# Moving a store ahead of y in one in-order queue of transfers

One core of a Trainium2 chip runs the kernel. The metric is the device time of that core in microseconds (us); lower is better.

## The reference

```python
def setup_inputs():
    batch, m, k, n = 16, 512, 768, 1024
    return {"x": randn(batch, k, m), "y": randn(batch, k, n)}   # float32

def reference(x, y):
    return np.einsum('bkm,bkn->bmn', x, y).astype(np.float32)
```

Sixteen products of a 512 x 768 by a 768 x 1024 matrix: 75.5 MB are read and 33.55 MB written.

## The kernel before

One batch entry is a round. The sync engine issues all transfers; VectorE casts x and y to bf16; PE multiplies (48 matmuls in two groups); ScalarE copies each group out of PSUM.

```python
LAG = 4          # the store of round b - 4 is issued in round b
NO = 5           # output buffers; xs, ys, xb, yb and the PSUM groups have two each
...
def store(b):
    if b < B - 2:
        nc.sync.wait_ge(groups, 2 * (b + 2))      # matmuls of round b + 1 done
    else:
        nc.sync.wait_ge(outs, b - (B - 3))        # copies of round b done
    nc.sync.dma_start(o_v[b], ob[b % NO][:]).then_inc(so[b % NO], 16)

for b in range(B):
    i = b % 2
    if b >= 2:
        nc.sync.wait_ge(cast, nx[b - 2])          # x of round b - 2 cast: its buffer is free
    wide_dma("x", xs[i][:], x_v[b], 4, True).then_inc(sx[i], 16)
    if b >= 2:
        nc.sync.wait_ge(cast, nx[b - 2] + parts(b - 2))
    wide_dma("y", ys[i][:], y_v[b], 2, True).then_inc(sy[i], 16)
    if b >= LAG:
        store(b - LAG)
for b in range(B - LAG, B):
    store(b)
...
# VectorE, round b
    if b >= 2:
        nc.vector.wait_ge(groups, 2 * (b - 1))    # xb and yb of round b - 2 read
    nc.vector.wait_ge(sx[i], n)
    nc.vector.tensor_copy(xb[:, i], xs[i][:]).then_inc(cast, 1)
    nc.vector.wait_ge(sy[i], n)
    nc.vector.tensor_copy(yb[:, i], ys[i][:]).then_inc(cast, 1)   # the last y in two halves
...
# ScalarE, round b, group g (cut here: from b = 5 on it first waits until the store of round b - 5 has landed)
    nc.scalar.wait_ge(groups, 2 * b + g + 1)
    cp = nc.scalar.copy(ob[b % NO][:, ...], ps[g][:])             # the last one releases the last store
```

Of the kernel before, what the change touches and what calls it, by code (L numbers as in the profile page):

```python
# [1 line left out]

_os.environ.setdefault("NEURON_RT_ULTRASERVER_MODE", "4")

# [2 lines left out]

# [5 lines left out]


@with_exitstack
def kernel(
    ctx: ExitStack,
    tc: tile.TileContext,
    x: bass.AP,
    y: bass.AP,  # L20
    out: bass.AP,
):
    nc = tc.nc
    P = 128
    FP32 = mybir.dt.float32
    BF16 = mybir.dt.bfloat16

    B, K, M = x.shape
    _, _, N = y.shape
    KT = K // P  # L30
    MT = M // P
    NF = 512
    NT = N // NF



    x_v = x.rearrange("b (p ko) m -> b p ko m", ko=KT)
    y_v = y.rearrange("b (p ko) n -> b p ko n", ko=KT)
    o_v = out.rearrange("b (p mo) n -> b p mo n", mo=MT)

    LAG = 4
    NO = 5
    KH = KT // 2

    ctx.enter_context(tc.tile_critical())
    ec = ctx.enter_context
    xs = [ec(nc.sbuf_tensor(f"xs{i}", [P, KT, M], FP32)) for i in range(2)]
    ys = [ec(nc.sbuf_tensor(f"ys{i}", [P, KT, N], FP32)) for i in range(2)]
    xb = ec(nc.sbuf_tensor("xb", [P, 2, KT, M], BF16))
    yb = ec(nc.sbuf_tensor("yb", [P, 2, KT, N], BF16))  # L50
    ob = [ec(nc.sbuf_tensor(f"ob{i}", [P, MT, N], FP32)) for i in range(NO)]

    HB = MT // 2
    ps = [ec(nc.psum_tensor(f"ps{i}", [P, HB, NT, NF], FP32)) for i in range(2)]
    sx = [ec(nc.semaphore(f"sx{i}")) for i in range(2)]
    sy = [ec(nc.semaphore(f"sy{i}")) for i in range(2)]
    so = [ec(nc.semaphore(f"so{i}")) for i in range(NO)]
    cast = ec(nc.semaphore("cast"))
    ready = ec(nc.semaphore("ready"))
    room = ec(nc.semaphore("room"))  # L60
    groups = ec(nc.semaphore("groups"))
    idle = ec(nc.semaphore("idle"))
    outs = ec(nc.semaphore("outs"))


    made = {}

    def wide_dma(key, dst, src, dram_rows, load):


        if key not in made:
            made[key] = nc.sync.dma_start(dst, src)
            return made[key]
        pat = mybir.BassSymbolicTensorAccessPattern
        widen = lambda a: a.rearrange("(q r) k m -> q (r k m)", r=dram_rows)
        plain = lambda a: a.rearrange("p k m -> p (k m)")
        s, d = (widen(src), plain(dst)) if load else (plain(src), widen(dst))
        return nc.sync.add_instruction(_copy.replace(
            made[key].ins, name=nc.get_next_instruction_name(),
            ins=(pat(ap=s.ap, dtype=s.dtype, bass_ap=s, is_dma=False),),  # L80
            outs=(pat(ap=d.ap, dtype=d.dtype, bass_ap=d, is_dma=False),),
            sync_info=None, ant_dge_precooked=False))


    def parts(b):
        return 2 if b in (15,) else 1


    nx = [sum(1 + parts(a) for a in range(b)) + 1 for b in range(B)]


    def store(b):


        if b < B - 2:
            nc.sync.wait_ge(groups, 2 * (b + 2))
        else:
            nc.sync.wait_ge(outs, b - (B - 3))
# [4 lines that stand above are left out]
        if b >= 2:  # L103
            nc.sync.wait_ge(cast, nx[b - 2])
        wide_dma("x", xs[i][:], x_v[b], 4, True).then_inc(sx[i], 16)
        if b >= 2:
            nc.sync.wait_ge(cast, nx[b - 2] + parts(b - 2))
        wide_dma("y", ys[i][:], y_v[b], 2, True).then_inc(sy[i], 16)
        if b >= LAG:
            store(b - LAG)  # L110
    for b in range(B - LAG, B):
        store(b)


    for _ in range(60):
        nc.vector.sem_inc(idle, 1)
    for b in range(B):
        i = b % 2
        n = 16 * (b // 2 + 1)
        if b >= 2:  # L120
            nc.vector.wait_ge(groups, 2 * (b - 1))
# [3 lines that stand above are left out]
        for h in range(parts(b)):  # L125
            ks = slice(h * KT // parts(b), (h + 1) * KT // parts(b))
            nc.vector.tensor_copy(yb[:, i, ks], ys[i][:, ks]).then_inc(cast, 1)  # L127


    for b in range(B):  # L130
        nc.gpsimd.wait_ge(cast, nx[b]).then_inc(ready, 1)
        for h in range(parts(b)):
            nc.gpsimd.wait_ge(cast, nx[b] + h + 1).then_inc(ready, 2 // parts(b))


    x_w = xb[:].rearrange("p s k (j mo) -> p s k mo j", mo=MT)
    pe = OrderedEngineSet([nc.tensor.engine])
    with nc.Fori(0, B // 2, engines=pe):
        with nc.Fori(0, 2, engines=pe) as s:
            nc.tensor.wait_ge(ready, 2).then_inc(ready, -2)  # L140
            for mo in range(MT):
                g, m = divmod(mo, HB)
                if m == 0:
                    nc.tensor.wait_ge(room, 1).then_inc(room, -1)  # L144
                for kt in range(KT):
                    if mo == 0 and kt == KH:
                        nc.tensor.wait_ge(ready, 1).then_inc(ready, -1)
                    for nt in range(NT):
                        mm = nc.tensor.matmul(  # L149
                            ps[g][:, m, nt], x_w[:, bass.ds(s, 1), kt, mo],  # L150
                            yb[:, bass.ds(s, 1), kt, nt * NF:(nt + 1) * NF],
                            start=(kt == 0), stop=(kt == KT - 1))
                if m == HB - 1:
                    mm.then_inc(groups, 1)


    nc.scalar.nop().then_inc(room, 2)
    for _ in range(60):
        nc.scalar.sem_inc(idle, 1)
    for b in range(B):  # L160
        if b >= NO:
            nc.scalar.wait_ge(so[b % NO], 16 * (b // NO))
        for g in range(2):
            nc.scalar.wait_ge(groups, 2 * b + g + 1)
            cp = nc.scalar.copy(ob[b % NO][:, g * HB:(g + 1) * HB].rearrange("p m (t f) -> p m t f", f=NF),  # L165
                                ps[g][:])
            if b < B - 1:
                cp.then_inc(room, 1)
        if b == B - 2:
            nc.scalar.drain().then_inc(outs, 1)  # L170
    cp.then_inc(outs, 1)

    for i in range(NO):
        nc.sync.wait_ge(so[i], 16 * len(range(i, B, NO)))


# [1 line left out]
_INS = ['x', 'y']  # L178
_OUTS = [((16, 512, 1024), 'float32')]


# [23 lines left out]
```

## Time and profile before

| | before |
|---|---|
| median time, first comparison | 262.54 us (262.36 to 262.94, 4 runs) |
| span of the profiled run | 260.2 us |
| share of the 16 DMA engines' span | 98.3% |
| busy PE / VectorE / ScalarE | 72% / 32% / 23% |
| last y lands / last copy ends / end | 234.7 / 251.2 / 260.2 us |

The order of issue of one middle round, from the timeline of the sync engine in the kernel before (start us, us, engine, line, operation):

```profile
181.84 0.47 SPq L72 DMA_DIRECT2D xs<-in_x_dram  x1
190.66 0.47 SPq L72 DMA_DIRECT2D ys<-in_y_dram  x1
191.18 0.59 SPq L99 DMA_DIRECT2D out_dram<-ob  x1
```

The store follows y at once: its own wait was over when the matmuls of round 11 ended, at 187.58 us.

### The profile page before, as it was taken

What the parts mean: (1) busy time and instruction counts of PE and PEld (TensorE: products, weight loads), DVE (VectorE), ACT (ScalarE), POOL (GpSimd) and SP (SyncE); (2) the same over time, 40 slices, a digit from 0 to 9 for tenths busy, and PEclk for the clock granted to TensorE, in tenths of its full rate; (3) what the DMA queues carried; (4) which work ended last, traced back from release to release, by engine and by line L of the source; (5) the groups of instructions that cost most, each with busy time, mean ns of one, the idle gap of its engine ahead of it and who ended that gap; (6) DMA issues with size and microseconds to landing.
All of it is one profiled execution on the core that took longest, in us unless ns stands there. A gap on an engine that the chain in (4) does not pass through costs nothing. (4 is left out here: it accounts for less than half of the span.)

```text
span 260.2 us, 2506 instructions
## 1 busy us (share of the span) xinstructions
PE 188.3 (72%) x768; PEld 90.3 (35%) x768; DVE 82.0 (32%) x33; ACT 61.1 (23%) x33; POOL 0.2 (0%) x4
## 2 busy tenths in 40 slices
PE   0019999998938959499491995949869697785930
PEld 0004555554513525244250352514424243442410
DVE  0261644525241152511425214252232523125000
ACT  1000442243220222203222022220412204031220
POOL 0000000000000000000000000000000000000000
PEclk9999999999995979979999597997968989997985
DMA  7999989999999999999999999999999999999995
GB/s 272 418 476 408 476 378 469 393 368 461 438 398 469 388 479 423 411 441 393 458 431 441 433 388 464 408 436 446 396 456 418 464 416 423 451 385 431 438 403 227
DMA packets 4514, 109.07 MB, mean 419 GB/s; under 512 B 768, under 2 KB 768, under 8 KB 768
## 3 DMA queue, kind: packets, MB, share of 16 engines
q1 hardware_dynamic: 4512, 109.05, 98.3%
q14 instruction: 2, 0.02, 0.0%
HBM read 75.50 MB, written 33.55 MB: 419 GB/s over the span
## 5 line engine op out<-in xcount | busy, mean ns | idle before, releaser
L149 PE MATMUL ps<-yb,xb 128*128 x768 | 188.3, 411 | 61.0 <-PEq L144 61.0
L149 PEld LDWEIGHTS ps<-yb,xb 128*128 x768 | 90.3, 118 | 158.5 <-issue 92.6
L165 ACT COPY ob<-ps 128x2048 f32<-128x2048 f32 x32 | 59.8, 1869 | 184.8 <-PE ps L149 184.8
L127 DVE CAST yb<-ys 128x6144 bf16<-128x6144 f32 (+1 forms) x17 | 53.8, 3171 | 86.5 <-DMA ys<-in_y_dram 86.5
L123 DVE CAST xb<-xs 128x3072 bf16<-128x3072 f32 x16 | 28.2, 1760 | 69.7 <-DMA xs<-in_x_dram 65.2
L165 ACT ACT_TABLE_LOAD x1 | 1.3, 1283 | 5.3 <-issue 5.3
L189 POOL MEMSET const-bfloat16-1.0<- 128x1 bf16 x1 | 0.1, 102 | 0.0
L189 POOL MEMSET const-uint8-127<- 128x1 uint8 x1 | 0.1, 102 | 0.0
L189 POOL MEMSET const-float32-1.0<- 128x1 f32 x1 | 0.1, 99 | 0.0
L189 POOL MEMSET const-float32-0.0<- 128x1 f32 x1 | 0.1, 98 | 0.2 <-issue 0.2
## 6 DMA issues: line engine op xcount, KB each, us to landing
ys<-in_y_dram SPq DMA_DIRECT2D x16, 3072.0 KB, 28.2
out_dram<-ob SPq DMA_DIRECT2D x16, 2048.0 KB, 32.6
xs<-in_x_dram SPq DMA_DIRECT2D x16, 1536.0 KB, 29.8
```

The costliest lines, as they stand in the source:

```text
L123: nc.vector.tensor_copy(xb[:, i], xs[i][:]).then_inc(cast, 1)
L127: nc.vector.tensor_copy(yb[:, i, ks], ys[i][:, ks]).then_inc(cast, 1)
L149: mm = nc.tensor.matmul(ps[g][:, m, nt], x_w[:, bass.ds(s, 1), kt, mo], yb[:, bass.ds(s, 1), kt, nt * NF:(nt + 1) * NF], start=(kt == 0), ...
L165: cp = nc.scalar.copy(ob[b % NO][:, g * HB:(g + 1) * HB].rearrange("p m (t f) -> p m t f", f=NF), ps[g][:])
L189: nc = _bacc.Bacc("TRN2", target_bir_lowering=False, num_devices=1)
```

## The change

The intent is to let the store go as soon as its data is there, between x and y, rather than behind y's wait for a free buffer.

```diff
         wide_dma("x", xs[i][:], x_v[b], 4, True).then_inc(sx[i], 16)
+        if LAG <= b < B - 1:
+            store(b - LAG)
         if b >= 2:
             nc.sync.wait_ge(cast, nx[b - 2] + parts(b - 2))
         wide_dma("y", ys[i][:], y_v[b], 2, True).then_inc(sy[i], 16)
-        if b >= LAG:
+        if b == B - 1:
             store(b - LAG)
```

## The prediction

> **What bounds the kernel now.** I read the page's DMA rows first, because a core that moves 109 MB in 260 us is suspected of being bound by transfers.
>
> ```profile
> DMA  7999989999999999999999999999999999999995
> q1 hardware_dynamic: 4512, 109.05, 98.3%
> HBM read 75.50 MB, written 33.55 MB: 419 GB/s over the span
> ```
>
> All 48 transfers go through one queue, and their packets occupy the 16 DMA engines for 98.3% of the span. Only the first and the last slice are visibly lower. PE is busy 72%, DVE 32%, ACT 23%: none is close. The chain that ended last holds only the last 48 matmuls (12.25 us) and one copy (1.87 us), because it doesn't follow queued transfers; I don't take it for the bound.
>
> Next, whether the queue ever runs dry. The issue table has the time from issue to landing:
>
> ```profile
> ys<-in_y_dram SPq DMA_DIRECT2D x16, 3072.0 KB, 28.2
> out_dram<-ob SPq DMA_DIRECT2D x16, 2048.0 KB, 32.6
> xs<-in_x_dram SPq DMA_DIRECT2D x16, 1536.0 KB, 29.8
> ```
>
> A transfer is issued about 30 us before it lands. A round (one x, one y, one store: 1.573 + 3.146 + 2.097 = 6.816 MB) takes 15.8 us, so nearly two rounds wait in the queue. The sync engine's waits for casts (115.8 us for y, 66.7 us for x) are therefore harmless: they hold up issues, not data. Stretches that begin where y landed, and three at the end, confirm it (columns: length, busy time of the five engines, granted clock, DMA share, GB/s):
>
> ```profile
> core 0: us, PE busy (x) PEld busy (x) DVE busy (x) ACT busy (x) POOL busy (x), PEclk, DMA share, GB/s
> 171.46:187.27 15.81, 12.02 (x49) 5.73 (x48) 5.12 (x2) 3.74 (x2) 0.00 (x0) 0.89 1.00 432
> 187.27:203.08 15.81, 12.23 (x45) 5.32 (x44) 5.12 (x3) 3.73 (x2) 0.00 (x0) 0.78 1.01 432
> ...
> 250.00:251.00 1.00, 0.00 (x0) 0.00 (x0) 0.00 (x0) 1.00 (x1) 0.00 (x0) 1.00 0.99 426
> 251.00:252.00 1.00, 0.00 (x0) 0.00 (x0) 0.00 (x0) 0.19 (x1) 0.00 (x0) 0.78 0.65 279
> 252.00:257.00 5.00, 0.00 (x0) 0.00 (x0) 0.00 (x0) 0.00 (x0) 0.00 (x0) 0.50 0.99 419
> ```
>
> The steady rounds run at share 1.00 and 432 GB/s. The one hole after the start-up is at 251 us: share 0.65, some 0.35 us lost. That is where the last store is issued. The timeline of the last two rounds:
>
> ```profile
> 211.68 1.76 DVE L123 CAST xb<-xs 128x3072 bf16<-128x3072 f32 x1 [5.24 <-DMA xs<-in_x_dram]
> ...
> 218.90 3.36 DVE L127 CAST yb<-ys 128x6144 bf16<-128x6144 f32 x1 [5.46 <-DMA ys<-in_y_dram]
> ...
> 222.83 10.55 PE L149 MATMUL ps<-yb,xb 128*128 x48 [3.63 <-PEq L144]
> 227.50 1.76 DVE L123 CAST xb<-xs 128x3072 bf16<-128x3072 f32 x1 [5.24 <-DMA xs<-in_x_dram]
> ...
> 237.05 12.23 PE L149 MATMUL ps<-yb,xb 128*128 x48 [3.67 <-PEq L144]
> ...
> 249.33 1.87 ACT L165 COPY ob<-ps 128x2048 f32<-128x2048 f32 x1 [3.25 <-PE ps L149]
> ```
>
> The start of a cast is here the landing of its input. The last y lands at 234.7; five stores of 4.99 us remain, ready in time except the last, issued at 251.2 when the last copy ends, just about when the queue runs out. So the kernel is bound by bytes throughout, and the last matmuls and copy are all but co-critical.
>
> [...] 432 in a steady round, and y alone at 3.146 MB / 7.22 us = 436. [...] x, y, store land in the order of issue. [...] in the trace 48 matmuls after a gap take 10.55 us in 2 rounds of 11, about 12.2 in 6, and 13.1 to 13.5 in 3, the granted clock falling to 0.50 for some microseconds.
>
> **The change part by part.** It adds and removes no instruction: 16 x, 16 y and 16 stores remain, each of the same shape. For rounds 4 to 14 it moves 11 stores from behind y to ahead of y. Round 15 and the last four stores keep their order.
>
> 1. Bytes and switches. Still 109.05 MB. The queue went x y s x y s; it becomes x s y x s y, still one group of loads and one store in turn, the same number of changes of direction. Gain: 0.
>
> 2. Issue waits. The store of round b-4 waits for the matmuls of round b-3. Now y of round b stands behind that wait. Take times relative to the landing of x of round b-2. From x to y are 7.22 us, from y to the next x 8.60; the x part of that is 3.61 at y's rate, so a store takes 4.99. In the new order y lands at 4.99 + 7.22 = 12.21, its cast ends at 15.57, and the next y may be issued. Matmuls of a round start some 0.5 us after y's cast (222.26 to 222.83) and take at most 13.5, so those of round b-3 end by 15.57 + 0.5 + 13.5 - 15.82 = 13.8. The store goes at 11 to 13.8, ahead of 15.57: it costs y no issue time. Issue to landing of y remains about 28 us, so even a missed microsecond would be hidden. Cost: 0.
>
> 3. Buffers. y and hence the matmuls come 5 us later in each middle round. The x cast of round b needs the matmuls of round b-2 finished: by 29.6 against a landing at 31.64 (two rounds). At worst 2.0 us are left. The output buffers are freed no later than before. Cost: 0.
>
> 4. First store. It waits until 41.74 in the trace; y4 was issued at 40.29 and is now issued behind it, at about 42.2. y3 landed at 47.89 and x4 after it, so y4 has more than 5 us in hand. Cost: 0.
>
> 5. The end. Up to y of round 15 the same bytes are ahead of it, so it again lands at 234.7. But y14 lands at 218.90 + 4.99 = 223.89, its cast ends at 227.25 (just before x15 lands at 227.50), and round 14's matmuls start at about 227.8 instead of 222.83. They end at 238.4, 240.0 or 241.2 with 10.55, 12.2 or 13.4 us. Round 15 was ready at 237.05; now it waits for PE, starts without a gap and at full clock (two copies lie 5.18 us apart in the early, uninterrupted rounds: 10.37 us for 48). It ends at 248.8, 250.4 or 251.6, and with 1.87 us of copy the last store is issued at 250.7, 252.3 or 253.5, against 251.2.
>
> Its landing takes 7.7 us in the trace, some of it behind the store before it. With an empty queue I estimate [...] 1.6 from the last byte (about 257.3) to landing (258.9): 7.0 us. So the end moves by -0.35 at best (the hole, which is all that can be filled), by +0.4 to +1.1 in the middle case, by +1.6 to +2.3 in the worst. Weighted 2:6:3 with centres -0.3, +0.75 and +1.95: about +0.9 us.
>
> Sum: 0 + 0 + 0 + 0 + 0.9 on 262.55 gives 263.4. [...] y periods now vary from 15.81 to 16.17 us between 75 and 171 us (about 1.4 us in all) for a reason I don't see; that could come out either way. I say 263.2.
>
> **Rivals.** (a) The store, now earlier, evens out the traffic and removes those 1.4 us and the hole: 260.8. For it: the rounds at 15.81 show the rate that is possible. Against: the share stays 1.00 in the slow rounds too, and reads and writes alternate as before. [...]
> (b) The store's wait for PE blocks the queue: each round PE's end, y's issue and the next matmuls would form a loop, and a round would lose microseconds, 11 rounds of 1 us making 273. For it: the chain y, matmuls, store, y is now in one queue. Against: step 2, with nearly 30 us between issue and landing; the loop spans two rounds and has slack.
> (c) PE slips past its slack [...] and the end is as in the worst case of step 5: 264.7.
>
> **Range and chances.** The middle is fixed by bytes, the tail may give -0.35 to +2.3, and the unexplained variation is worth about 1.4 either way: 261.6 to 265.0. A change of 2% is 5.25 us; [...] slower needs (b). 0.02, 0.94, 0.04.
>
> **What would show it.** Right: queue share near 98%, period of x landings 15.8 to 16.0, x to y about 12.2 and y to x about 3.6 us, y15 landing near 234.7, rounds 14 and 15 back to back on PE, the last store issued at 250.7 to 253.5 and a deeper hole before it if late. Wrong: DMA share below 0.95 in a middle round, issue to landing of y well under 20 us, or steady rounds whose rate differs from 432 GB/s though the queue is full.

What no trace of this case showed is cut above, where it is marked. In step 5 two terms of the last store's landing on an empty queue, with the 1.6 us, came to 7.0 us, and the +0.9 us of step 5, the sum of 263.4 and the point of 263.2 us were reckoned with the two; these were the author's assumption. The trace of before has 0.64 us from the end of the first issue (1.34 us) to the first packet (1.98 us), and at the 436 GB/s of y alone 2.097 MB take 4.81 us. What sets the granted clock of a round is not shown (after a gap of 3.63 us 48 matmuls took 10.55 us at a clock of 1.00, after one of 3.58 us 13.38 us at 0.78).

Two readings of the trace of before that the prediction uses, with their figures: all 48 transfers land in the order of issue (the last part of each; the first of them at 7.20 us, the last at 258.93 us), and "full clock" in step 5 is the granted clock of 1.00 from 26.22 to 62.43 us, where PE has no gap.

## The result and the profile after

| first comparison | before | after |
|---|---|---|
| median of 4 runs, us | 262.54 | 263.20 (263.03 to 263.59) |
| ratio (95% interval) | | 1.0025 (1.0008 to 1.0042) |
| last y's cast starts | 234.72 | 236.15 |
| last copy ends | 251.20 | 251.93 |
| span | 260.2 | 261.6 |

A ratio is the mean time of one kernel's fast runs over that of the other's of the same rounds, so it is not quite the ratio of the medians quoted.

The page of the kernel after: its span, the DMA rows, and the issue table with the time from issue to landing.

```profile
span 261.6 us, 2506 instructions
...
DMA  6998999999999999989999998999999999999994
...
q1 hardware_dynamic: 4512, 109.05, 97.9%
...
ys<-in_y_dram SPq DMA_DIRECT2D x16, 3072.0 KB, 28.2
out_dram<-ob SPq DMA_DIRECT2D x16, 2048.0 KB, 24.1
xs<-in_x_dram SPq DMA_DIRECT2D x16, 1536.0 KB, 29.8
```

By these times the queue is as full as before: y and x wait in it as long as before (28.2 and 29.8 us). The store waits 8.5 us less (32.6 to 24.1), as it now waits for PE on the issuing engine instead of in the queue: the sync engine's waits for PE ahead of stores add up to 130.2 us, against 26.8 before. A middle round on the sync engine, kernel after:

```profile
183.09 0.47 SPq L72 DMA_DIRECT2D xs<-in_x_dram  x1
193.73 0.34 SPq L99 DMA_DIRECT2D out_dram<-ob  x1
196.77 0.47 SPq L72 DMA_DIRECT2D ys<-in_y_dram  x1
```

The last rounds, from the timeline of the kernel after. The start of a cast is the landing of its input (the last y lands at 236.13 us, its cast starts at 236.15), except where VectorE was still busy.

```profile
213.07 1.76 DVE L125 CAST xb<-xs 128x3072 bf16<-128x3072 f32 x1 [0.46 <-DMA xs<-in_x_dram]
...
225.18 3.36 DVE L129 CAST yb<-ys 128x6144 bf16<-128x6144 f32 x1 [10.35 <-DMA ys<-in_y_dram]
...
228.94 1.76 DVE L125 CAST xb<-xs 128x3072 bf16<-128x3072 f32 x1 [0.40 <-DMA xs<-in_x_dram]
229.11 20.91 PE L151 MATMUL ps<-yb,xb 128*128 x96 [3.74 <-PEq L146]
...
236.15 3.43 DVE L129 CAST yb<-ys 128x3072 bf16<-128x3072 f32 x2 [5.46 <-DMA ys<-in_y_dram]
...
250.06 1.87 ACT L167 COPY ob<-ps 128x2048 f32<-128x2048 f32 x1 [3.26 <-PE ps L151]
```

x to y is now 12.11 us and y to the next x 3.76. The matmuls of rounds 14 and 15 form one piece of 96, at a granted clock of 1.00. All that is as predicted. What is not: the last y lands 1.43 us later than in the trace of before, and from there to the end it is 25.45 us against 25.48 before (the span is printed to 0.1 us, so both are good to 0.05). So the whole difference of the two traces arose before the last y landed, where the prediction had put nothing, and none of it after, where it had put +0.9 us.

Where it arose is in the records of single packets in the trace. A load packet of 49,152 bytes takes 1.83 us in the median (before, 1,440 packets). The last load packet ahead of the first store takes longer on every one of the 16 DMA engines, up to 2.85 us before and 3.13 us after. Later switches from loads to stores cost single engines some 0.1 to 0.6 us. The cast of y starts when the last of its 16 parts has landed (in the trace of before 234.70 and 234.72 us), so the engine furthest behind decides. The 16 parts of one y land within about 1.1 us of each other in each of the first four rounds; once stores begin the engines drift apart, and for the last y it is 2.56 us before and 3.47 us after. So the 16 engines finish their parts of one transfer up to 3.5 us apart.

### The profile page after: what moved, and what is told of

It reads as the page before. It is cut to its first block, busy times and chain, and to the rows that moved or that the text cites. A ratio compares the mean times of both kernels' runs of the same rounds, so it can differ in the third digit from the quotient of the medians.

```text
span 261.6 us, 2506 instructions
## 1 busy us (share of the span) xinstructions
PE 190.3 (73%) x768; PEld 90.5 (35%) x768; DVE 82.0 (31%) x33; ACT 61.1 (23%) x33; POOL 0.2 (0%) x4
## 5 line engine op out<-in xcount | busy, mean ns | idle before, releaser
L151 PE MATMUL ps<-yb,xb 128*128 x768 | 190.3, 414 | 59.8 <-PEq L146 59.7
L125 DVE CAST xb<-xs 128x3072 bf16<-128x3072 f32 x16 | 28.2, 1760 | 18.0 <-DMA xs<-in_x_dram 15.0
## 6 DMA issues: line engine op xcount, KB each, us to landing
ys<-in_y_dram SPq DMA_DIRECT2D x16, 3072.0 KB, 28.2
out_dram<-ob SPq DMA_DIRECT2D x16, 2048.0 KB, 24.1
xs<-in_x_dram SPq DMA_DIRECT2D x16, 1536.0 KB, 29.8
```

The costliest lines, as they stand in the source:

```text
L151: mm = nc.tensor.matmul(ps[g][:, m, nt], x_w[:, bass.ds(s, 1), kt, mo], yb[:, bass.ds(s, 1), kt, nt * NF:(nt + 1) * NF], start=(kt == 0), ...
```

## The experiments

The first theory: the change makes the loss at the switch from loads to stores larger, and the tail (step 5 of the prediction) plays no part. Rivals: the tail; chance.

### The two kernels again

No edit. Expected of before:

> The kernel before, unchanged: how much of what the two traces differ in is chance. Ratio 1.000 within 0.15%. Theory 'loss at the switch' (in the trace of before the last load packet ahead of a store takes up to 1 us longer than its 1.83 us, and the 16 DMA engines drift apart until their landings of one transfer are 2.6 us apart; after: 3.5 us) expects the last y to land near 234.7 us again and the spread to settle near 2.5 us. Rival 'chance': last y anywhere between 234.5 and 236.5.

Expected of after:

> The changed kernel again. Ratio 1.0025 (1.001 to 1.004). Theory 'loss at the switch': last y lands near 236.1 us again (1.4 later than before), spread near 3.5 us, and 24.2 us from there to the end as in before. Rival 'the tail' (the prediction's step 5: the last store is issued too late): last y at 234.7 and a longer tail, by 0.4 to 1.1 us. Rival 'chance': last y anywhere between 234.5 and 236.5.

Measured: before 262.54 us, ratio 0.9992 (0.9977 to 1.0006); after 262.54 us, ratio 0.9995 (0.9977 to 1.0013). The cast of the last y, before again and then after again:

```profile
235.82 3.43 DVE L127 CAST yb<-ys 128x3072 bf16<-128x3072 f32 x2 [5.46 <-DMA ys<-in_y_dram]
```

```profile
235.37 3.43 DVE L129 CAST yb<-ys 128x3072 bf16<-128x3072 f32 x2 [5.46 <-DMA ys<-in_y_dram]
```

The order is reversed: in this pair the kernel before lands its last y later. (The 24.2 us in these expectations count up to the last landing, which comes 1.2 us before the end of the span.) The landing spread of the last y is 3.45 us (before) and 2.91 us (after). My theory that the change makes the drift larger falls in its strong form; most of the 1.43 us was chance. The remainder holds: 25.48 and 25.43 us from the last y to the end.

### The change in some rounds only

Shown shortened, against the changed kernel.

```diff
-        if LAG <= b < B - 1:              # and the complement behind y
+        if b >= LAG and b < 8:            # first: rounds 4 to 7
+        if 8 <= b < B - 1:                # second: rounds 8 to 14
+        if b >= LAG and b == B - 2:       # third: round 14 only
```

> Stores go between x and y in rounds 4 to 7 only. Theory 'loss at the switch, early': all of the change's loss is there, last y near 236 us, time +0.6 us (ratio 1.0025). Theory 'the tail': no change (1.000), as the last rounds are those of before.

> Stores go between x and y in rounds 8 to 14 only. Theory 'loss at the switch, early': engines have mostly drifted apart by then, so +0.0 to +0.3 us (1.000 to 1.001), last y near 234.7 to 235. Theory 'the tail': the whole of the difference, +0.65 us (1.0025) with a last y at 234.7.

> Only the store issued in round 14 goes between x and y. Matmuls of rounds 14 and 15 then run back to back, the last store is issued about 0.5 us earlier to 2 us later, as in step 5 of the prediction. Step 5 expects +0.4 to +1.1 us (+0.9 in the mean, ratio 1.0035). Theory 'loss at the switch' expects 1.000: the DMA engine that is furthest behind still has some 1 to 1.5 us of the store before it to move when the last one is issued, so the last y at 234.7 and the tail of 24.2 us stay.

Measured: 1.0004 (0.9989 to 1.0018), 1.0004 (0.9990 to 1.0017) and 1.0011 (0.9998 to 1.0025). No group of rounds carries a loss that shows, though intervals this wide could hide 0.1%. The third run tests step 5 alone, for it has the tail of the changed kernel. Its span, the cast of its last y and its last copy:

```profile
span 260.3 us, 2506 instructions
...
234.90 3.43 DVE L129 CAST yb<-ys 128x3072 bf16<-128x3072 f32 x2 [5.46 <-DMA ys<-in_y_dram]
...
250.13 1.87 ACT L167 COPY ob<-ps 128x2048 f32<-128x2048 f32 x1 [3.25 <-PE ps L151]
```

The last copy ends 17.1 us after the last y lands, 0.6 us later than before, and the end comes 25.4 us after it, as before. Rounds 8 to 14 give 17.46 and 25.5 us. The last store was issued later, and the end did not move.

### Does VectorE disturb the switch?

In the changed kernel VectorE casts y just while the last x packets ahead of a store move (at the first switch from 48.01 to 51.37 us, the packets from 48.23 to 52.48 us); before, it is idle when the last y packets move (0.00 us busy from 55.40 to 59.30 us). First the changed kernel with that cast held back, then the kernel before with VectorE kept busy.

```diff
         nc.vector.wait_ge(sy[i], n)
+        if LAG - 1 <= b < 12:
+            nc.vector.wait_ge(sx[1 - i], 16 * ((b + 1) // 2 + 1))
```

```diff
+        for _ in range(3 if b >= LAG else 0):
+            nc.vector.tensor_copy(xb[:, i], xs[i][:])
+            nc.vector.drain()
         nc.vector.tensor_copy(xb[:, i], xs[i][:]).then_inc(cast, 1)
```

> The changed kernel; in rounds 3 to 11 the cast of y waits until the next x has landed, so VectorE is idle while the last x packets ahead of a store move (in the changed kernel it casts y just then). Theory 'VectorE disturbs the switch': the loss falls to that of before: last y near 234.7, ratio 1.000. Rival 'it is x ahead of the store, whatever VectorE does': as the changed kernel, last y near 236.1, 1.0025.

> The kernel before; from round 4 on VectorE casts x four times in a row (7 us instead of 1.8), so that it is busy while the last y packets ahead of a store move. Nothing waits for the additional casts. Theory 'VectorE disturbs the switch': loss as in the changed kernel or above, last y near 236, ratio 1.0025 or more. Rival 'x ahead of the store': as before, 1.000.

Measured: 1.0006 (0.9991 to 1.0021) and 1.0000 (0.9987 to 1.0013), last y at 234.7 and 235.0 us. The second speaks against the theory: 7 us of casts in each round cost nothing. The first fits it by its last y, 0.5 us ahead of the earliest of the changed kernel's three traces, but the profiled run is the fastest of its six and the ratio is no lower than 1. VectorE isn't shown to matter.

### Half as many switches

```diff
-        if b >= LAG:
-            store(b - LAG)
+        if b > LAG and b % 2:
+            store(b - LAG - 1)
+            store(b - LAG)
```

> The kernel before with two stores after every second y, so half as many switches from loads to stores (stores of rounds 0 and 1 behind y of round 5, and so on). Theory 'loss at the switch': the first switch costs the same, the later ones half: last y 0.5 to 1 us earlier relative to its bytes, time 261.5 to 262.2 (0.996 to 0.999). Rival 'switches cost nothing': 1.000.

Measured: 261.88 us against 262.41, ratio 0.9987 (0.9973 to 1.0001), not clear of 1. In its trace the prolonged load packets add up to 0.37 us per engine, against 1.19 us before. But from the seventh store on its stores land 4.86 to 5.07 us apart on the engine furthest behind, where in the kernel before the last nine take 4.80 to 4.88. That these longer steps take back some of the 0.82 us is an estimate from these figures.

### The last store made late on purpose

The very last copy is made three times, so that the last store is released later. Kernel before otherwise.

```diff
             if b < B - 1:
                 cp.then_inc(room, 1)
+            elif g == 1:
+                nc.scalar.drain()
+                cp = nc.scalar.copy(...)      # the same copy
+                nc.scalar.drain()
+                cp = nc.scalar.copy(...)      # and again
```

> The kernel before, with the very last copy made three times, so that the last store is issued 3.8 to 4 us later, some 20.2 us after the last y lands. So far it has been issued 15.0 to 17.5 us after it with no effect on the end. Theory 'slack': the slowest DMA engine needs it only from 17.5 to 18.5 us on, so the end comes 1.7 to 2.7 us later (ratio 1.006 to 1.010). Prediction's step 5 ('no slack, 0.35 us at most'): 3.5 to 4 us later (1.013 to 1.015). Rival 'hidden however late': 1.000.

Timed: 1.0015 (0.9995 to 1.0035), less than expected; its four runs go from 262.37 to 265.0 us, and the profiled one is the slowest. That run shows the mechanism. Its page begins

```profile
span 263.2 us, 2510 instructions
```

Its timeline has the cast of the last y and the last copy:

```profile
235.37 3.43 DVE L127 CAST yb<-ys 128x3072 bf16<-128x3072 f32 x2 [5.46 <-DMA ys<-in_y_dram]
...
253.84 1.87 ACT L174 COPY ob<-ps 128x2048 f32<-128x2048 f32 x1
```

And stretches of 2 us (length, busy time of the engines, clock, DMA share, GB/s):

```profile
252.00:254.00 2.00, 0.00 (x0) 0.00 (x0) 0.00 (x0) 1.93 (x2) 0.00 (x0) 0.61 0.12 49
254.00:256.00 2.00, 0.00 (x0) 0.00 (x0) 0.00 (x0) 1.70 (x1) 0.00 (x0) 0.50 0.00 0
256.00:258.00 2.00, 0.00 (x0) 0.00 (x0) 0.00 (x0) 0.00 (x0) 0.00 (x0) 0.50 0.93 393
```

Here the queue is truly empty: share 0.00 for 2 us. The end comes 263.2 - 235.37 = 27.83 us after the last y, 2.4 us later than in all the others. From the end of the last copy to the end of the span it is 263.2 - 255.71 = 7.49 us when the queue is empty. An undisturbed end comes 25.4 to 25.5 us after the last y, so the last copy may end up to 18.0 us after it (25.45 - 7.49) at no cost. The runs that aren't profiled show no such detail; the runs near 262.4 must have released the store earlier, which is only argued. PE may be the reason: the last 48 matmuls take 12.23 us in this trace and 10.72 in that of the run with VectorE busy, and 1.5 us less would leave a delay of some 0.9 us (an estimate).

Compare with the changed kernel around the end of its last copy, at 251.93 us:

```profile
251.00:252.00 1.00, 0.00 (x0) 0.00 (x0) 0.00 (x0) 0.92 (x1) 0.00 (x0) 1.00 0.84 360
252.00:253.00 1.00, 0.00 (x0) 0.00 (x0) 0.00 (x0) 0.00 (x0) 0.00 (x0) 1.00 0.74 311
253.00:254.00 1.00, 0.00 (x0) 0.00 (x0) 0.00 (x0) 0.00 (x0) 0.00 (x0) 1.00 0.73 311
```

There is a hole (0.84, 0.74, 0.73), but it costs nothing. The share is the mean over 16 engines: some have run out while the one furthest behind is still busy with the store before, and the end waits for that one.

The landing records show it, independently of the 18.0 us. In every trace of the table below the first part of the last store lands 6.1 to 6.2 us after the last copy ends: its engine waited for nothing but the issue. The last part lands later by 1.60 us before, by 2.31, 0.75 and 0.63 us in the three traces of after, and by 0.16 us with the late copy, where all engines had run dry. That lateness is the slack that was left. It agrees with 18.0 less the first column of the table within 0.2 us in each of the ten traces whose copy ends before 18.0.

| trace | last copy ends, us after last y lands | end, us after last y lands |
|---|---|---|
| before / again | 16.48 / 16.47 | 25.48 / 25.48 |
| after / again / third | 15.78 / 17.36 / 17.45 | 25.45 / 25.43 / 25.39 |
| rounds 4 to 7 / 8 to 14 / 14 only | 16.48 / 17.46 / 17.10 | 25.49 / 25.50 / 25.40 |
| cast held back / VectorE busy | 15.77 / 14.96 | 25.40 / 25.46 |
| last copy three times | 20.34 | 27.83 |

("Lands" is the start of y's cast; the end is that of the span, printed to 0.1 us, so 25.39 and 25.50 don't clearly differ.)

### How long a wait the queue hides

The changed kernel, with each moved store, and so y behind it, waiting for PE one or two rounds longer:

```diff
-            nc.sync.wait_ge(groups, 2 * (b + 2))
+            nc.sync.wait_ge(groups, 2 * (b + 2 + more))   # more = 1 or 2, moved stores only
```

> The changed kernel; each moved store waits for the matmuls of one more round, so y stands behind a wait that ends 16 us later. Step 2 of the prediction (the queue's depth hides issue waits): issue to landing of y falls from 28 to about 15 us, the time stays, 1.000. Rival (b) (the wait delays data): the loss shows already, 1.01 or more.

> The same with two more rounds: now the store of round b-4 and y of round b are issued only when the matmuls of round b-1 are done, with nothing left in the queue. Here rival (b) must come true if step 2 is right about why it does not in the changed kernel: [...] 29 to 31 us in place of 15.8 for 11 rounds: 405 to 430 us, ratio 1.55 to 1.65. If waits never matter: 1.00.

The terms of the loop are cut here, as not all of them were read from a trace; they came to the 29 to 31 us that stand.

Measured: one more round 269.48 us, 1.0274 (1.0220 to 1.0328); two more 423.66 us, 1.6149 (1.6100 to 1.6199). The issue tables, one more and then two more:

```profile
ys<-in_y_dram SPq DMA_DIRECT2D x16, 3072.0 KB, 16.2
out_dram<-ob SPq DMA_DIRECT2D x16, 2048.0 KB, 9.5
```

```profile
ys<-in_y_dram SPq DMA_DIRECT2D x16, 3072.0 KB, 14.2
out_dram<-ob SPq DMA_DIRECT2D x16, 2048.0 KB, 7.2
```

Two more came out as expected: in its trace one turn of the loop takes 30.71 us, 14.58 from the store's issue at 216.33 us to the start of y's cast, 3.89 to the first matmul at 234.80, 12.24 to the next store's issue at 247.04. So the loop of rival (b) is real once the queue can't hide it. One more I expected at 1.000, and it missed. I had looked at y alone, which indeed fell to 16.2 us. But the store is the first transfer to be issued after the wait, and its issue to landing is 9.5 us. An empty queue gives 7.2, so it had 2.3 us in hand in the median, and in some rounds none. The first moved store shows it, in a stretch of the kernel with one more round:

```profile
51.00:54.00 3.00, 3.00 (x16) 1.58 (x14) 2.00 (x2) 1.66 (x1) 0.00 (x0) 1.00 0.41 175
```

The share falls to 0.41. In the changed kernel the same figure is 24.1 us, 17 us above that of an empty queue, so the shift of a few microseconds that the change makes is well hidden.

### The changed kernel a third time

> The changed kernel a third time: the first comparison gave 1.0025 (1.0008 to 1.0042), the second 0.9995 (0.9977 to 1.0013). Theory 'no difference; the slowest DMA engine's drift is chance': 1.000 within 0.0015. Rival 'a small real loss of 0.25%': 1.0025, above 1.001.

Measured: 262.92 us against 262.43, ratio 1.0015 (1.0002 to 1.0029), between the two theories. The three comparisons are 1.0025, 0.9995 and 1.0015, with a mean of 1.0012, or 0.3 us.

Is that 0.3 us real? From the packet records I took the load packets prolonged at the first switch and divided their excess over 1.83 us by 16 engines:

```text
x ahead of the first store (after, again, third, rounds 4-7, cast held back): 0.89 0.62 0.85 0.96 0.76 us
y ahead of the first store (before, again, round 14, VectorE busy, late copy, rounds 8-14): 0.64 0.68 0.40 0.59 0.56 0.27 us
```

The means are 0.82 and 0.52 us, a difference of the right size. But I looked for it after the fact, the groups overlap, the run with paired stores (y ahead, 0.33) is left out, and no run was made to test it. So a loss of some 0.1% is possible and not shown; nor is there a cause for the loss at a switch itself. Both stay open.

## Why the prediction was right, and where it was not

**"Same", and the range.** The kernel is bound by bytes, the change moves none, and the time stayed within 0.3% in every comparison. That is the reason given, and it held. That the point of 263.2 equals the first median to the digit is luck: the repeat gave 262.54.

**Step 1, bytes and switches: 0.** Right to within the 0.3 us left open. Load packets at the switches are prolonged in both orders (up to 2.85 us before and 3.13 us after, in place of 1.83), and the number of switches is the same; whether that costs the kernel time isn't shown (half as many gave 0.9987, not clear of 1).

**Step 2, issue waits: 0.** Right. y is still issued 28.2 us before it lands, as predicted. The reasoning looked at the wrong member, though. What must be early enough is the first transfer behind the wait, the store; "nearly 30 us" should have been 24.1 less 7.2. The run with one more round of wait was predicted by the same reasoning and missed by 2.7%.

**Step 3, buffers: 0.** Right: x to y 12.11 us where 12.21 was predicted, and in the last rounds x's cast starts on landing or as soon as y's cast is done.

**Step 4, the first store: 0.** y4 was issued at 41.93 (predicted 42.2) and nothing ran dry there (DMA share 0.99 from 41.9 to 57.7 us). The load packets ahead of the first store were prolonged, by up to 1.3 us on one engine in the trace of after, but that happens in both orders.

**Step 5, the end: +0.9.** This step failed. Its first half was right: rounds 14 and 15 ran back to back (96 matmuls in 20.91 us, at a granted clock of 1.00), and the last store was released at 251.9, 252.7 and 252.7 us in the three traces, where 250.7 to 253.5 was predicted. Its second half said that the last matmuls and copy are "all but co-critical" and that the queue runs out "just about" as the last store is issued, so that each microsecond of delay counts. In fact the last copy ended 16.48 us after the last y where up to 18.0 us are free: 1.5 us of slack. The changed kernel used 15.78 to 17.45 us in its three traces, and the term is 0 in each. The error was to read a mean share of 0.65 as a hole in the queue; it was a hole on the engines that were ahead. The prediction's own numbers speak against it. Five stores of 4.99 us after 234.7 land the last one at 259.7, while 251.2 plus its 7.0 for an empty queue is 258.2, so by these figures 1.5 us were free.

That 7.0 is too long as well: in the run with the late copy the last store takes 6.3 us from issue to landing. The 1.6 from last byte to landing was counted from 257.3, where the mean share falls; from the end of the last packet on any engine (258.56) to the landing (258.93) it is 0.4. From the end of the first issue to the first packet it is 0.64 us (before).

**What stood in for it.** The prediction saw that y periods vary, allowed 1.4 us either way, and could not name a reason. That was the term that set the two traces of the first comparison apart: the last y landed anywhere from 234.7 to 236.2 us in the eleven traces of the table above, and the two orders overlap: 234.7 (before) to 235.8 (before again) with stores behind y, 234.7 (cast held back) to 236.2 (after) with stores ahead of it. It goes with the drift of the DMA engines: over these traces the first part of the last y lands within 0.7 us, the spread to the last part goes from 2.30 to 3.62 us, and the late ones are mostly those with a wide spread (correlation 0.91). In each trace the spread of y keeps one value over the first four rounds, between 0.8 and 1.4 us, and grows once stores begin. That the switches themselves cause the drift is likely, not shown.

**Rivals.** (a) needed the hole to be worth something; it was not. (b) needs two more rounds of wait to come true, and starts with one. (c) did not occur in three traces; its 253.5 us would lie 18.8 us after the last y, past the free 18.0 by 0.8 us and not by the 1.6 to 2.3 that were worked out.

## What to carry to other kernels

Here one full in-order queue was the bound (98.3% of the 16 DMA engines' span), and reordering its transfers changed nothing that shows (1.0025, 0.9995 and 1.0015) until the queue ran dry (1.0274 and 1.6149). In such a kernel, measure how far from dry it is as issue to landing less that of an empty queue, for the first transfer behind each wait. A mean DMA share below 1 doesn't show that the critical DMA engine is idle (shares of 0.65 before and 0.73 after cost nothing here): compare the distance from a landing to the end in several traces. And repeat a difference of a quarter of a per cent before explaining it.
